# A hybrid attention/SSD trunk on one core: three projection units at the start instead of two, and three value units placed between the convolved projection groups

## The chip, the cores and the metric

One core of one Trainium2 chip runs the whole kernel. The metric is device time in microseconds (us) of one execution, the median of several runs. The engines are named as in the profile: PE is TensorE (PEld its weight loads), DVE is VectorE, ACT is ScalarE, POOL is GpSimd, SP issues the DMAs.

## What is computed

One layer of a streaming encoder for two groups of tokens that share the weights: 512 prompt tokens and 32 sample tokens, 544 in all, model width 1024. In float32:

```
h = rmsnorm(x)
[q, k, v | z, xBC, dt | gate_a, gate_b] = h @ w_in
ya = QK-normed chunk-band attention(q, k, v)
xBC = silu(causal depthwise conv of width 4 over xBC);  dt = softplus(dt + dt_bias)
yb = rmsnorm( SSD scan(xBC, dt) * silu(z) )
x += (sigmoid(gate_a) * (ya @ w_proj_a) + sigmoid(gate_b) * (yb @ w_proj_b)) @ w_out
x += ConvFFN(rmsnorm(x));   x += sigmoid(rmsnorm(x) @ w_ple_gate) * (p @ w_ple)
```

The outputs are y, the new keys and values, the SSD states and the convolution contexts of both groups.

## The kernel before, in words

Activations lie feature-major: a tile has 128 features on the partitions and 544 tokens along the free dimension. The dense work is cut into **units**: one unit makes 128 output features from 1024 input features and reads one weight tile of 128x1024 (all weights are packed on the host in the order in which the units use them, two units to a 1 MB DMA, `load`, tile `wr`). A unit has 8 **chunks**, one for each 128 input features. To keep float32 accuracy from the fast matmul form, a weight is split into `wh` (rounded) and `wl` (the rest), an activation into `hi` and `lo`, and a chunk (`mm3`) is 6 matmuls of 128x128 by 128x272: wh by hi, wh by lo and wl by hi, each for two halves of the tokens. `prep` makes `wh` on ACT (a copy that rounds) and `wl` on DVE, or for odd units below 40 on POOL; `wh` and `wl` have two buffers each.

`dense_steps` is the list of units, 192 in all: B, C and four x units of each of four groups ("xbc", with a convolution behind them), z, then q, k and v of eight head pairs, the gates, the output projections, the FFN and the last projection. `Dense.chunk` runs the next chunk and, after a unit's eighth, its epilogue; `dense.run(n)` runs n chunks, and the small matmuls of the SSD scan and of attention are put between chunks by hand (`ssd_a`, `ssd_b`, `att_a`, `att_b`, `att_c`). `dense.defer(n, fn)` runs fn n chunks later. PE's order is pinned to the order in which the program is written (`Ordered._pin`); the order of the other engines is set by a scheduler, which is bound by true dependencies and by the few `add_manual_dep` calls. On the chip each engine works through its own list in that order.

The PSUM banks: `dps` (two banks, two buffers) takes a dense unit, `sps` (one bank, four buffers) everything else. So a unit can't start before the unit two ahead of it has been read out by its epilogue.

**The start.** x comes in as eight tiles (`load_x`, tile `xin`), with the weights of units 0 and 1 in pieces between them. `split_g` makes hi on ACT and lo on DVE (L374, L375), `prep_part` the pieces of wh and wl (L259, L260). The sum of squares for the first rmsnorm is made apart from that: tiles 0 to 3 are squared and added on POOL (L443, L445), tiles 4 to 7 are squared on ACT and added on DVE. `Dense.start` runs units 0 and 1 together, chunk by chunk as the x tiles come; then `rstd_of` sums over the partitions with a matmul by ones (tile `rps`) and makes 1/rms on ACT (Ln, then Exp). The norm is not applied to h but to each unit's result: `evac_ext` multiplies it out of PSUM by `rstd`. Then `dt_product` (32 small matmuls, tile `dtp`), and 8 chunks later `dt_softplus`, 32 chunks after that `dt_sums`, whose result goes to DRAM (`asc`) and comes back spread over the partitions (`ab`) for the SSD scan. `bias_vector` writes a vector of relative-position biases to DRAM (`evec`), and 16 DMAs `bsc` of 320 KB spread it for attention.

**Epilogues.** `ep_xbc`: three DVE reads of PSUM into `ext` (L571, L573, L574), a convolution of one ACT and three DVE operations (tile `cv`), a tanh on ACT (`th`) and two last DVE operations into `bc` or `xs`. `ep_v`: one DVE read of PSUM into `v`, a DMA of v to DRAM, and three chunks later (`v_transpose`) five PE transposes of v (tiles `vt`, `vs`) and their copies on ACT.

The functions that the change touches, and their callers:

Of the kernel before, what the change touches and what calls it, by code (L numbers as in the profile page):

```python
# [15 lines left out]
D = 1024  # L16
# [100 lines left out]
def trunk(ctx: ExitStack, tc: tile.TileContext, a):  # L117
# [109 lines left out]

    raws = {0: r0}
    ready = {}
    first_rstd = []  # L230
    used = set()
# [8 lines left out]
    def prep(u):  # L240
        if u >= len(order) or u in ready or u in used:
            return
        load(u // 2)
        r = raws[u // 2][:, u % 2, :]
        hi = wp.tile([128, 1024], F32R, tag="wh", name="wh", bufs=2)
        lo = wp.tile([128, 1024], F32R, tag="wl", name="wl", bufs=2)
        ready[u] = (hi, lo)
        if u < 2:
            return r
        cp = S.copy(hi, r)  # L250
        if u == 3:
            tc.add_manual_dep(cp.ins, first_rstd[0].ins.name, ORDER, reason="order")
        eng = G if u < 40 and u % 2 == 1 else V
        eng.tensor_tensor(lo, r, hi.bitcast(F32), op=SUB)  # L254
        load(u // 2 + 1)

    def prep_part(u, r, c0, c1):
        hi, lo = ready[u]
        S.copy(hi[:, c0:c1], r[:, c0:c1])  # L259
        V.tensor_tensor(lo[:, c0:c1], r[:, c0:c1], hi[:, c0:c1].bitcast(F32), op=SUB)  # L260

# [26 lines left out]
    class Dense:  # L288
# [47 lines left out]
        def start(self):  # L336
            sts = self.steps[:2]
            pss = [dps() for _ in sts]
            ws = [next_unit(*units_of(st)[0]) for st in sts]
            for n in range(KD):  # L340
                for st, ps, w in zip(sts, pss, ws):
                    o = 128 * n
                    mm3(ps, w[0][:, o : o + 128], w[1][:, o : o + 128], *acts_of[st[0]](st)[n], n == 0, n == KD - 1)
                    self.count += 1
            self.i = 2
            first_rstd.append(rstd_of(rstd, acc, 1.0 / D))
            for st, ps in zip(sts, pss):
                epilogue[st[0]](ps, *st[1:])
            dt_product()

# [15 lines left out]
    def split(x):  # L366
# [3 lines left out]
        return hi, lo  # L370

    def split_g(x, g):
        hi, lo = slot(F32R, "hi"), slot(F32R, "lo")
        S.activation(hi, x, AF.Copy, scale=g)  # L374
        V.scalar_tensor_tensor(lo, x, g, hi.bitcast(F32), op0=MUL, op1=SUB)  # L375
        return hi, lo
# [15 lines left out]
    def rstd_of(dst, acc, scale, after=None):  # L392
# [3 lines left out]
        for h in range(2):  # L396
# [8 lines left out]
            if pre is not None:  # L405
                tc.add_manual_dep(ln.ins, pre.ins.name, ORDER, reason="table")
        for h in range(2):
            sl = slice(h * HALF, (h + 1) * HALF)
            last = S.activation(dst[:, sl], dst[:, sl], AF.Exp, scale=-0.5)
        return last  # L410

# [4 lines left out]
    for k in range(KD):  # L416
        hx.append(split_g(xt[k], vec[:, V_GMIX + k : V_GMIX + k + 1]))
        if k in (0, 1, 3):
            for u in range(2):
                prep_part(u, rw[u], (0, 256, 0, 512)[k], (256, 512, 0, 1024)[k])  # L420
    load(1)
    nc.sync.dma_start(hb, a["hb"].unsqueeze(0).to_broadcast([128, 2, 32]))
# [27 lines left out]
    done(acc2)  # L450
    rstd = big("rstd")
# [21 lines left out]
    def dt_product():  # L473
# [8 lines left out]
        for h in range(2):  # L482
            sl = slice(h * HALF, (h + 1) * HALF)
            V.tensor_tensor(dtx[:, sl], ps[h][:, :HALF], rstd[:, sl], op=MUL)
        dense.defer(8, lambda: dt_softplus(dtx))

    def dt_softplus(dtx):
# [23 lines left out]
        dt = tm[:, 0]  # L511
        V.scalar_tensor_tensor(dt, p, 2.0, x, op0=MUL, op1=ADD)
# [6 lines left out]
    def dt_sums(dtx, ws, r, dt, agf):  # L519
        cp = sps("cum")  # L520
# [761 lines left out]
```

## Time and profile before

| | |
|---|---|
| median of 3 runs | 1355.56 us (1354.17 to 1358.21) |
| the profiled execution | 1355.77 us |
| its span, first to last instruction | 1354.1 us |
| PE busy | 1338.2 us (99% of the span) |
| DVE, ACT, POOL busy | 852.6, 634.4, 313.7 us |
| granted TensorE clock, mean | 0.999 |
| idle PE time by the waits' view | 11.1 us in ten groups of waits, 4.1 us of it for `lo` at the start |

A row of a timeline view gives the start (us), the duration (us; of the whole merged group), the engine, the line and the operation, and in brackets how long the engine was idle before it and who ended that. A busy PE is not PE at its peak: its rows overlap, and the pace is read from the distance of their starts. The other engines' rows overlap a little too (by about 0.1 us).

### The profile page before, as it was taken

How to read it: one execution, taken by the hardware profiler on the slowest of the kernel's cores; microseconds unless marked ns; L12 is line 12 of the kernel's file. 1: busy time of each engine (PE TensorE's matmuls, PEld its weight loads, DVE VectorE, ACT ScalarE, POOL GpSimd, SP SyncE). 2: the span in 40 equal slices, each digit the busy share in tenths (PEclk: the TensorE clock that was granted, in tenths of full speed). 3: DMA queues.
4: the chain of work that ended last, by engine and by line, in shares of the span. 5: the costliest groups of instructions: out<-in, count | busy, mean ns of one | idle time of the engine just before them, and what ended most of it. 6: DMA issues, size and time to landing. Idle time of an engine off the chain costs nothing.

```text
span 1354.1 us, 26563 instructions
## 1 busy us (share of the span) xinstructions
PE 1338.2 (99%) x11045; PEld 1307.2 (97%) x11045; DVE 852.6 (63%) x1474; ACT 634.4 (47%) x1104; POOL 313.7 (23%) x442
## 2 busy tenths in 40 slices
PE   8999999999999999999999999999999999999998
PEld 7999998999999999999999999999999999999998
DVE  7999889755775656643554335677676356753545
ACT  5465555656676667542442223534444124432342
POOL 5456365544321211100000000133332013310000
PEclk9999999999999999999999999999999999999999
DMA  5733243332533332222223422222222232222231
GB/s 182 252 100 130 83 128 121 119 132 100 177 94 114 115 111 90 67 81 94 69 89 110 143 94 73 85 94 94 94 72 85 94 111 94 76 85 94 94 107 53
DMA packets 41896, 142.15 MB, mean 105 GB/s; under 512 B 9216, under 2 KB 13232, under 8 KB 29488
## 3 DMA queue, kind: packets, MB, share of 16 engines
q1 hardware_dynamic: 41776, 140.45, 31.4%
q8 instruction: 87, 1.43, 0.4%
q14 instruction: 33, 0.27, 0.1%
HBM read 129.27 MB, written 14.31 MB: 106 GB/s over the span
## 4 chain that ended last, share of the span: by engine, by line
PE 89%; DVE 6%; ACT 2%; DMA 1%; issue 1%; SPq 0%; POOL 0%; ACTq 0%; DVEq 0%; POOLq 0%
PE dps L130 80%; PE O L130 2%; PE yps L130 2%; PE L L130 1%; PE st L130 1%; DVE cv L599 1%; DVE qs L834 1%; PE Tp L133 1%; DVE wl L254 1%; PE xst L133 0%; PE gps L130 0%; DMA wr<-in_w 0%; DVE xs L603 0%; DMA ab<-asc 0%; PE qn L130 0%
## 5 line engine op out<-in xcount | busy, mean ns | idle before, releaser
L130 PE MATMUL dps<-hi,wh 128*128 128x272 f32 x2960 | 627.0, 293 | 0.6 <-DVE ext L574 0.4
L130 PE MATMUL dps<-lo,wh 128*128 128x272 f32 x2960 | 613.1, 288 | 4.1 <-DVE lo L375 4.1
L130 PE MATMUL dps<-hi,wl 128*128 128x272 f32 x2960 | 612.1, 288 | 0.0
L130 PEld LDWEIGHTS dps<-hi,wh 128*128 128x128 f32 x2960 | 466.0, 189 | 10.5 <-issue 7.8
L130 PEld LDWEIGHTS dps<-lo,wh 128*128 128x128 f32 x2960 | 465.9, 189 | 5.0 <-DVE lo L375 5.0
L130 PEld LDWEIGHTS dps<-hi,wl 128*128 128x128 f32 x2960 | 464.9, 188 | 0.0
L250 ACT CAST wh<-wr 128x1024 fp32r<-128x1024 f32 x192 | 201.2, 1048 | 386.0 <-PE dps L130 346.6
L254 DVE TENSOR_TENSOR wl<-wr,wh 128x1024 fp32r<-128x1024 f32 x173 | 213.6, 1235 | 47.6 <-ACT wh L250 42.3
L1033 DVE SCALAR_TENSOR_TENSOR ucv<-uext,vec,ucv 128x546 f32<-128x546 f32 x96 | 75.3, 784 | 4.4 <-ACT ucv L1030 2.7
L599 DVE SCALAR_TENSOR_TENSOR cv<-ext,hv,cv 128x547 f32<-128x547 f32 x72 | 71.0, 986 | 2.1 <-ACT cv L596 1.0
L1026 POOL COPY cfo<-uext 128x2 f32<-128x2 f32 x48 | 10.4, 217 | 261.7 <-DVE uext L573 261.7
L1023 POOL MEMSET uext<- 128x2 f32 x48 | 4.5, 95 | 278.7 <-issue 278.7
L1065 DVE TENSOR_TENSOR x<-x,dps 128x544 f32<-128x544 f32 x24 | 17.3, 721 | 78.0 <-PE dps L130 78.0
L571 DVE TENSOR_TENSOR uext<-dps,rstd 128x272 f32<-128x272 f32 x48 | 21.3, 443 | 63.0 <-PE dps L130 58.3
L785 DVE CUSTOM_DVE_ANT_0 P<-L,bias 128x128 f32<-128x128 f32 (+3 forms) x64 | 30.8, 481 | 46.1 <-PE L L130 41.6
L254 POOL TENSOR_TENSOR wl<-wr,wh 128x1024 fp32r<-128x1024 f32 x19 | 48.4, 2549 | 43.9 <-ACT wh L250 42.4
L1027 POOL COPY cfo<-uext 128x2 f32<-128x2 f32 x48 | 55.5, 1157 | 0.0
L787 ACT ACTIVATE P<-P,sm 128x128 f32<-128x128 f32 (+3 forms) x64 | 36.0, 562 | 26.8 <-DVE sm L785 26.4
L660 POOL TENSOR_TENSOR ab<-ab,bc 128x512 f32<-128x512 f32 (+1 forms) x28 | 37.0, 1325 | 40.7 <-ACT ab L659 40.7
L368 ACT CAST hi<-me 128x544 fp32r<-128x544 f32 x24 | 15.5, 647 | 61.9 <-DVE me L1051 61.9
L1030 ACT ACTIVATE ucv<-uext,vec 128x546 f32<-128x546 f32 x48 | 40.7, 847 | 7.2 <-DVE uext L574 2.6
L650 ACT ACTIVATE m<-ab,tm 128x128 f32<-128x128 f32 x128 | 40.8, 389 | 6.3 <-DMA ab<-asc 6.2
(243 smaller groups left out, 1548.9 us busy)
## 6 DMA issues: line engine op xcount, KB each, us to landing
wr<-in_w SPq DMA_DIRECT2D x96, 1024.0 KB, 4.9
ab<-asc SPq DMA_DIRECT2D x32, 256.0 KB, 5.1
bsc<-evec SPq DMA_DIRECT2D x16, 320.0 KB, 8.0
bias<-bsc SPq DMA_DIRECT2D x16, 256.0 KB, 3.2
xin<-in_xT SPq DMA_DIRECT2D x8, 272.0 KB, 5.7
out_o_v<-v SPq DMA_DIRECT2D x8, 272.0 KB, 3.2
out_o_k<-qk SPq DMA_DIRECT2D x8, 272.0 KB, 2.9
x<-in_xT SPq DMA_DIRECT2D x8, 272.0 KB, 4.4
```

The costliest lines, as they stand in the source:

```text
L130: return self._pin(nc.tensor.matmul(*args, **kw))
L250: cp = S.copy(hi, r)
L254: eng.tensor_tensor(lo, r, hi.bitcast(F32), op=SUB)
L571: V.tensor_tensor(ext[:, n : n + HALF], ps[:, 0, :HALF], rstd[:, 0:HALF], op=MUL)
L599: V.scalar_tensor_tensor(y[:, :n], ext[:, j : j + n], hv[:, 24 * j + ti : 24 * j + ti + 1], y[:, :n], op0=MUL, op1=ADD)
L650: S.activation(m[:, i], ab[:Q, i], AF.Relu, scale=-1.0, bias=tm[:Q, 1, c, hd : hd + 1])
L660: G.tensor_tensor(ab, ab, cc[:, tk].unsqueeze(1).to_broadcast([128, H, Q]), op=MUL)
L785: V.tensor_tensor_reduce(out=P, in0=L, in1=B, scale=1.0, scalar=3e38, op0=ADD, op1=MIN, accum_out=nm[:n])
L787: S.activation(P, P, AF.Exp, scale=-1.0, bias=nm[:n], accum_out=sm[:n])
L1027: G.tensor_copy(cfo[:, i, 2:4], ext[:, UW - 2 : UW])
L1030: S.activation(y[:, :n], ext[:, 0:n], AF.Identity, scale=vec[:, V_FW + i : V_FW + i + 1], bias=vec[:, V_FB + i : V_FB + i + 1])
L1033: V.scalar_tensor_tensor(y[:, :n], ext[:, j : j + n], vec[:, V_FW + 48 * j + i : V_FW + 48 * j + i + 1], y[:, :n], op0=MUL, op1=ADD)
```

## The change

- **Third unit at the start.** `Dense.start` takes three units. Units 0 and 1 run chunk by chunk as before; all 8 chunks of unit 2 follow. Unit 2's weights come with the second weight DMA (`r1`), now issued right behind the x tiles; its wh and wl have tiles of their own (`prep_third`), its sums two `sps` banks (`dpa`, `dpb`). The matmul `rps` of the norm stands behind the sixth chunk of unit 2.
- **Sum of squares.** All eight squares are on ACT and all sums on DVE, none on POOL; tile 0 is squared early, tiles 1 to 7 are ordered behind the split of unit 2's weights. That split is ordered behind the last x split.
- **Epilogues of units 0 to 2**: all three are read out of PSUM first, and then convolved.
- **Later work.** `dt_product` goes four chunks behind the start (it followed at once), `dt_softplus` 6 chunks after it (8), `dt_sums` 26 after that (32); the first operation of `bias_vector` is ordered behind the last one of `dt_softplus`. `wl` of unit 3 is made on DVE, not on POOL.
- **Order of units.** The value units of head pairs 0 and 1 are units 6 and 7, ahead of the second xbc group, that of pair 2 is unit 14, between the second and the third; z(0) comes behind the fourth xbc group. The counts at which the SSD scan and attention are put between the chunks stay.

The core of the diff:

```diff
@@ dense_steps
     def qkv(m):
-        return [("qk", m, 0), ("qk", m, 1), ("v", m)]
+        return [("qk", m, 0), ("qk", m, 1)] + [("v", m)] * (m >= 3)
...
-    p += proj(1) + proj(2) + z(0) + proj(3) + z(1)
+    p += v(0, 1) + proj(1) + v(2) + proj(2) + proj(3) + z(0) + z(1)
@@ loads
     for k in range(5, KD):
         load_x(k)
+    r1 = wp.tile([128, 2, 1024], F32, tag="wr", name="wr", bufs=2)
+    nc.sync.dma_start(r1, a["w"][1])
     nc.sync.dma_start(vec[:, V_BG:V_N], a["vec"][:, V_BG:V_N])
@@ prep
-        eng = G if u < 40 and u % 2 == 1 else V
+        eng = G if 3 < u < 40 and u % 2 == 1 else V
...
+    def prep_third():
+        third.extend(slot(F32R, n) for n in ("wh", "wh", "wl", "wl"))
+        ready[2] = Joined(*third[:2]), Joined(*third[2:])
+        return [prep_part(2, r1[:, 0, :], c, c + 512) for c in (0, 512)][-1]
@@ Dense.start
+            sts = self.steps[:3]
+            pss = [dps() for _ in range(2)]
...
+            pss.append(Banks(sps("dpa"), sps("dpb")))
...
+            seq = [(n, i) for n in range(KD) for i in range(2)] + [(n, 2) for n in range(KD)]
+            for j, (n, i) in enumerate(seq):
...
+                self.count += 1
+                if j == 21:
+                    rstd_of(rstd, acc, 1.0 / D)
+            done(*third)
+            self.i = 3
+            for f in [xbc_evac(ps, *st[1:]) for st, ps in zip(sts, pss)]:
+                f()
+            self.defer(4, dt_product)
@@ the sum of squares
+        if k == 0:
+            sq0 = S.activation(acc, xt[0], AF.Square)
+            tc.add_manual_dep(sq0.ins, part[0].ins.name, ORDER, reason="order")
+    last_w = prep_third()
+    tc.add_manual_dep(last_w[0].ins, last[0].ins.name, ORDER, reason="order")
...
-    acc2 = slot(name="acc2")
-    for k in range(KD):
-        if k < 4:
-            q = acc2 if k == 0 else eslot("sq")[:, :T]
-            G.tensor_tensor(q, xt[k], xt[k], op=MUL)
-            if k > 0:
-                G.tensor_tensor(acc2, acc2, q, op=ADD)
...
+    for k in range(1, KD):
+        q = eslot("sq")[:, :T]
+        sq = S.activation(q, xt[k], AF.Square)
+        add = V.tensor_tensor(acc, acc, q, op=ADD)
+        tc.add_manual_dep(sq.ins, last_w[0].ins.name, ORDER, reason="order")
+        tc.add_manual_dep(add.ins, last_w[1].ins.name, ORDER, reason="order")
@@ dt_product, dt_softplus, bias_vector
-        dense.defer(8, lambda: dt_softplus(dtx))
+        dense.defer(6, lambda: dt_softplus(dtx))
...
-        dense.defer(32, lambda: dt_sums(dtx, ws, r, dt, agf))
+        dense.defer(26, lambda: dt_sums(dtx, ws, r, dt, agf, last_dt))
...
+        neg = V.tensor_scalar(er[0:16, 0:257], er[0:16, 0:257], -1.0, None, op0=MUL)
+        tc.add_manual_dep(neg.ins, last_dt.ins.name, ORDER, reason="order")
```

`xbc_evac` is the first half of the old `ep_xbc` (up to the reads of PSUM), and returns the second (`xbc_conv`).

How the order of the engines changes, at the three places that the prediction speaks of. Line numbers of the changed program are some 2 to 37 higher than those of the program before.

DVE at the start, before: `lo` of an x tile, `wl` of units 0 and 1 and then of unit 2, the sums `acc`, up to the first read of a unit out of PSUM (`ext`).

```order
L375 SCALAR_TENSOR_TENSOR lo<-xin,vec,hi 128x544 x3
L384 TENSOR_TENSOR acc<-acc,sq 128x544
L459 TENSOR_SCALAR hv<-vec 128x120
L460 TENSOR_SCALAR hv<-vec 128x16
L461 TENSOR_SCALAR hv<-vec 128x1
L375 SCALAR_TENSOR_TENSOR lo<-xin,vec,hi 128x544
L448 TENSOR_TENSOR acc<-acc,acc_200 128x544
L375 SCALAR_TENSOR_TENSOR lo<-xin,vec,hi 128x544
L384 TENSOR_TENSOR acc<-acc,sq 128x544 x2
L254 TENSOR_TENSOR wl<-wr,wh 128x1024
L571 TENSOR_TENSOR ext<-dps,rstd 128x272
```

DVE at the start, now:

```order
L409 SCALAR_TENSOR_TENSOR lo<-xin,vec,hi 128x544 x5
L490 TENSOR_SCALAR hv<-vec 128x16
L491 TENSOR_SCALAR hv<-vec 128x1
L262 TENSOR_TENSOR wl<-wr,wh 128x512 x2
L477 TENSOR_TENSOR acc<-acc,sq 128x544 x5
L256 TENSOR_TENSOR wl<-wr,wh 128x1024
L477 TENSOR_TENSOR acc<-acc,sq 128x544
L256 TENSOR_TENSOR wl<-wr,wh 128x1024
L477 TENSOR_TENSOR acc<-acc,sq 128x544
L488 TENSOR_SCALAR hv<-vec 128x120
L602 TENSOR_TENSOR ext<-dps,rstd 128x272 x2
```

The five last `lo` stand together, `wl` of units 2 (two halves) and 3 and 4 (128x1024) stand between them and the last sums, and `ext` comes behind all of these.

PE at the third chunk behind unit 6, the first value unit, now (dps rows are dense matmuls, three rows to a chunk; `vt` and `vs` are the transposes of v, `cum` begins `dt_sums`):

```order
L133 MATMUL dps<-hi,wh 128x272 x2
L133 MATMUL dps<-lo,wh 128x272 x2
L133 MATMUL dps<-hi,wl 128x272 x2
L136 MATMUL vt<-ident,v 128x128 x4
L136 MATMUL vs<-ident,v 32x128
L133 MATMUL dps<-hi,wh 128x272 x2
L133 MATMUL dps<-lo,wh 128x272 x2
L133 MATMUL dps<-hi,wl 128x272 x2
L133 MATMUL cum<-dtt,tri 128x128
```

The transposes of v stood some 220 chunks later before; they now stand three chunks behind unit 6, one chunk ahead of `dt_sums`.

DVE ahead of the read of unit 6 (`v<-dps`), now (`dtt` and `tm` are the softplus, `er` and `e` the bias vector):

```order
L538 SCALAR_TENSOR_TENSOR dtt<-dtt 128x160
L636 SCALAR_TENSOR_TENSOR cv<-ext,hv,cv 128x547
L539 SCALAR_TENSOR_TENSOR dtt<-dtt 128x160
L636 SCALAR_TENSOR_TENSOR cv<-ext,hv,cv 128x547
L542 SCALAR_TENSOR_TENSOR tm<-dtt 128x160
L584 TENSOR_SCALAR er<-er 16x257
L256 TENSOR_TENSOR wl<-wr,wh 128x1024
L636 SCALAR_TENSOR_TENSOR cv<-ext,hv,cv 128x547
L545 SCALAR_TENSOR_TENSOR dtt<-tm,ea 128x160
L586 COPY e_899<-er 16x383
L800 TENSOR_TENSOR v<-dps,rstd 128x544
```

Behind the epilogues of units 0 to 5 and the whole softplus stands the read of v; before, the seventh read of a unit out of PSUM stood at this place, and no PE instruction but the second unit after it waited for that.

## Rows read from the trace of the kernel before

**Rows 1.** Who waited for whom on PE: total us, times, longest.

```profile
PE dps L130 <- DVE lo L375: 4.1, 3, 3.3
PE st L130 <- DVE xs L690: 1.8, 2, 1.2
```

**Rows 2.** Timeline of PE at the start.

```profile
16.15 0.55 PE L130 MATMUL dps<-lo,wh 128*128 128x272 f32 x2 [3.27 <-DVE lo L375]
...
20.05 0.41 PE L130 MATMUL dps<-lo,wh 128*128 128x272 f32 x2
...
25.07 1.08 PE L130 MATMUL rps<-acc,ones 128*128 128x272 f32 x4
26.08 2.04 PE L130 MATMUL dtp<-xin,dtw 128*32 128x272 f32 x32
...
34.67 1.15 PE L130 MATMUL tps<-sel,dtx 128*128 128x32 f32 x10
```

**Rows 3.** Stretches of 5 us: busy us (instructions) of each engine, PEclk, DMA share, GB/s.

```profile
15.00:20.00 5.00, 3.85 (x18) 3.85 (x19) 5.00 (x8) 2.11 (x5) 3.94 (x5) 0.66 0.99 383
```

**Rows 4.** Timeline of DVE at the start.

```profile
14.24 4.70 DVE L375 SCALAR_TENSOR_TENSOR lo<-xin,vec,hi 128x544 fp32r<-128x544 f32 x3
...
19.77 0.77 DVE L375 SCALAR_TENSOR_TENSOR lo<-xin,vec,hi 128x544 fp32r<-128x544 f32 x1
20.46 0.71 DVE L448 TENSOR_TENSOR acc<-acc,acc 128x544 f32<-128x544 f32 x1
...
25.35 1.23 DVE L254 TENSOR_TENSOR wl<-wr,wh 128x1024 fp32r<-128x1024 f32 x1 [2.01 <-ACT wh L250]
27.02 0.44 DVE L571 TENSOR_TENSOR ext<-dps,rstd 128x272 f32<-128x272 f32 x1 [0.45 <-ACT rstd L409]
```

**Rows 5.** Timeline of POOL at the start.

```profile
13.73 1.78 POOL L445 TENSOR_TENSOR acc<-acc,sq 128x544 f32<-128x544 f32 x1
```

**Rows 6.** Timeline of ACT at the start.

```profile
11.32 1.47 ACT L374 ACTIVATE hi<-xin,vec 128x544 fp32r<-128x544 f32 x2
...
13.87 0.64 ACT L383 ACTIVATE sq<-xin 128x544 f32<-128x544 f32 x1
...
24.27 1.05 ACT L250 CAST wh<-wr 128x1024 fp32r<-128x1024 f32 x1 [6.13 <-PE dps L130]
```

**Rows 7.** DMA issues of 11.3 to 11.6 us: operation, count, KB, us to landing.

```profile
wr<-in_w SPq DMA_DIRECT2D x1, 1024.0 KB, 6.4
```

**Rows 8.** Timeline of DVE from 28 to 59 us.

```profile
28.34 2.58 DVE L555 COPY e<-er 16x383 f32<-16x383 f32 x1
...
31.20 2.41 DVE L599 SCALAR_TENSOR_TENSOR cv<-ext,hv,cv 128x547 f32<-128x547 f32 x3
...
34.34 0.69 DVE L603 SCALAR_TENSOR_TENSOR bc<-th,cv 128x512 f32<-128x512 f32 x1
...
45.26 1.76 DVE L508 SCALAR_TENSOR_TENSOR dtt<-dtt 128x160 f32<-128x160 f32 x1
...
55.76 2.92 DVE L599 SCALAR_TENSOR_TENSOR cv<-ext,hv,cv 128x547 f32<-128x547 f32 x1
58.60 0.31 DVE L515 SCALAR_TENSOR_TENSOR dtt<-tm,ea 128x160 f32<-128x160 f32 x1
58.84 0.43 DVE L571 TENSOR_TENSOR ext<-dps,rstd 128x272 f32<-128x272 f32 x1
```

**Rows 9.** Timeline of POOL: a weight subtraction, the second of three before 58 us.

```profile
42.96 3.88 POOL L254 TENSOR_TENSOR wl<-wr,wh 128x1024 fp32r<-128x1024 f32 x1 [2.53 <-ACT wh L250]
```

**Rows 10.** Timeline of PE: `dt_sums` begins behind unit 6; an SSD wait.

```profile
59.96 0.56 PE L130 MATMUL cum<-dtt,tri 128*128 128x128 f32 x4
...
232.68 1.10 PE L130 MATMUL st<-wj,bt 128*128 128x512 f32 x2 [1.16 <-DVE xs L690]
```

**Rows 11.** Instructions on tile v, 28 to 345 us: ns min/median/max, first and last start.

```profile
L763 DVE TENSOR_TENSOR v<-dps,rstd x3: 723/724/725, 286.3 to 338.3; 128x544 f32<-128x544 f32 x3
```

**Rows 12.** Timeline of SP: the DMAs of the bias rows.

```profile
34.38 14.32 SPq L563 DMA_DIRECT2D bsc<-evec  x14
```

More of the change, by code (lines that the diff above doesn't have):

```diff
@@ L45, in qkv, with v @@
     def qkv(m):
-        return [("qk", m, 0), ("qk", m, 1), ("v", m)]
+        return [("qk", m, 0), ("qk", m, 1)] + [("v", m)] * (m >= 3)
+    def v(*ms):
+        return [("v", m) for m in ms]
     p = proj(0)
-    p += proj(1) + proj(2) + z(0) + proj(3) + z(1)
+    p += v(0, 1) + proj(1) + v(2) + proj(2) + proj(3) + z(0) + z(1)
     for m in range(NPAIR):
@@ L225, in trunk @@
     done(wz_t)
-    raws = {0: r0}
+    raws = {0: r0, 1: r1}
     ready = {}
-    first_rstd = []
     used = set()
@@ L249, in prep @@
             return r
-        cp = S.copy(hi, r)
-        if u == 3:
-            tc.add_manual_dep(cp.ins, first_rstd[0].ins.name, ORDER, reason="order")
-        eng = G if u < 40 and u % 2 == 1 else V
+        S.copy(hi, r)
+        eng = G if 3 < u < 40 and u % 2 == 1 else V
         eng.tensor_tensor(lo, r, hi.bitcast(F32), op=SUB)
@@ L258, in prep_part, with __init__, __getitem__ @@
         hi, lo = ready[u]
-        S.copy(hi[:, c0:c1], r[:, c0:c1])
-        V.tensor_tensor(lo[:, c0:c1], r[:, c0:c1], hi[:, c0:c1].bitcast(F32), op=SUB)
+        return (S.copy(hi[:, c0:c1], r[:, c0:c1]),
+                V.tensor_tensor(lo[:, c0:c1], r[:, c0:c1], hi[:, c0:c1].bitcast(F32), op=SUB))
+    class Joined:
+        def __init__(self, *t):
+            self.t = t
+        def __getitem__(self, k):
+            c0, c1 = k[1].start, k[1].stop
+            return self.t[c0 // 512][k[0], c0 % 512 : c0 % 512 + c1 - c0]
+    class Banks:
+        def __init__(self, *t):
+            self.t = t
+        def __getitem__(self, k):
+            return self.t[k[1]][k[0], k[2]]
+    third = []
+    def prep_third():
+        third.extend(slot(F32R, n) for n in ("wh", "wh", "wl", "wl"))
+        ready[2] = Joined(*third[:2]), Joined(*third[2:])
+        return [prep_part(2, r1[:, 0, :], c, c + 512) for c in (0, 512)][-1]
     pos = [0]
@@ L336, in start @@
         def start(self):
[L337 to L349, printed above, removed]
+            sts = self.steps[:3]
+            pss = [dps() for _ in range(2)]
+            ws = [next_unit(*units_of(st)[0]) for st in sts[:2]]
+            pss.append(Banks(sps("dpa"), sps("dpb")))
+            pos[0] += 1
+            used.add(2)
+            ws.append(ready.pop(2))
+            seq = [(n, i) for n in range(KD) for i in range(2)] + [(n, 2) for n in range(KD)]
+            for j, (n, i) in enumerate(seq):
+                w = ws[i]
+                o = 128 * n
+                mm3(pss[i], w[0][:, o : o + 128], w[1][:, o : o + 128], *acts_of[sts[i][0]](sts[i])[n], n == 0,
+                    n == KD - 1)
+                self.count += 1
[6 more added lines that the diff above has]
+            self.defer(4, dt_product)
         def run(self, n):
@@ L370, in split @@
         return hi, lo
+    last = []
     def split_g(x, g):
         hi, lo = slot(F32R, "hi"), slot(F32R, "lo")
-        S.activation(hi, x, AF.Copy, scale=g)
-        V.scalar_tensor_tensor(lo, x, g, hi.bitcast(F32), op0=MUL, op1=SUB)
+        last[:] = (S.activation(hi, x, AF.Copy, scale=g),
+                   V.scalar_tensor_tensor(lo, x, g, hi.bitcast(F32), op0=MUL, op1=SUB))
         return hi, lo
@@ L406, in rstd_of @@
                 tc.add_manual_dep(ln.ins, pre.ins.name, ORDER, reason="table")
[L407 to L410, printed above, removed]
+            S.activation(dst[:, sl], dst[:, sl], AF.Exp, scale=-0.5)
     hx = []
@@ L419, in trunk @@
             for u in range(2):
-                prep_part(u, rw[u], (0, 256, 0, 512)[k], (256, 512, 0, 1024)[k])
-    load(1)
+                part = prep_part(u, rw[u], (0, 256, 0, 512)[k], (256, 512, 0, 1024)[k])
+        if k == 0:
[3 more added lines that the diff above has]
+    tc.add_manual_dep(last_w[0].ins, last[0].ins.name, ORDER, reason="order")
     nc.sync.dma_start(hb, a["hb"].unsqueeze(0).to_broadcast([128, 2, 32]))
@@ L458, in trunk @@
     hv = const.tile([128, 138], F32, name="hv")
-    V.tensor_scalar(hv[:, 0:120], vec[:, V_CW : V_CW + 120], 0.5, None, op0=MUL)
+    hv0 = V.tensor_scalar(hv[:, 0:120], vec[:, V_CW : V_CW + 120], 0.5, None, op0=MUL)
+    tc.add_manual_dep(hv0.ins, add.ins.name, ORDER, reason="order")
     V.tensor_scalar(hv[:, 120:136], vec[:, V_BG : V_BG + 16], 0.5, None, op0=MUL)
@@ L511, in dt_softplus @@
         dt = tm[:, 0]
-        V.scalar_tensor_tensor(dt, p, 2.0, x, op0=MUL, op1=ADD)
+        last_dt = V.scalar_tensor_tensor(dt, p, 2.0, x, op0=MUL, op1=ADD)
         ea = const.tile([128, 32], F32, name="ea")
@@ L516, in dt_softplus, with dt_sums @@
         agf = ag.rearrange("p c h -> p (c h)")
-        dense.defer(32, lambda: dt_sums(dtx, ws, r, dt, agf))
-    def dt_sums(dtx, ws, r, dt, agf):
+        dense.defer(26, lambda: dt_sums(dtx, ws, r, dt, agf, last_dt))
+    def dt_sums(dtx, ws, r, dt, agf, last_dt):
         cp = sps("cum")
@@ L548, in dt_sums, with bias_vector @@
         done(dtx, *ws)
-        dense.defer(4, bias_vector)
-    def bias_vector():
+        dense.defer(4, lambda: bias_vector(last_dt))
+    def bias_vector(last_dt):
         er, e0 = slot(name="er"), slot(name="e0")
         nc.sync.dma_start(er[0:16, 0:257], a["rb"])
-        V.tensor_scalar(er[0:16, 0:257], er[0:16, 0:257], -1.0, None, op0=MUL)
+        neg = V.tensor_scalar(er[0:16, 0:257], er[0:16, 0:257], -1.0, None, op0=MUL)
+        tc.add_manual_dep(neg.ins, last_dt.ins.name, ORDER, reason="order")
         V.tensor_copy(e0[0:16, 0:383], er[0:16, 0:1].to_broadcast([16, 383]))
@@ L580, in ep_xbc, with xbc_evac @@
     def ep_xbc(ps, kind, i):
+        xbc_evac(ps, kind, i)()
+    def xbc_evac(ps, kind, i):
         if kind == "x":
@@ L593, in ep_xbc, with xbc_conv @@
         G.tensor_copy(cso[:, ti, 3:6], ext[:, XW - 3 : XW])
+        return lambda: xbc_conv(ext, ti, dst)
+    def xbc_conv(ext, ti, dst):
         n = XW - 3
```

5 lines of the change are left out of this document (removed).

## The prediction

> **What bounds the kernel now.** PE is busy for 99% of the span (the page's first section), so a change can only give back, or add, idle PE time, or time at a low clock. The first view to read is therefore who waited for whom on PE: the largest entry is 4.1 us for `lo` at the start, the next 1.8 us for `xs` of the SSD scan [rows 1]. The timeline of PE shows the first in place: one wait of 3.27 us ahead of 16.15 us [rows 2]. Behind it the nine pairs of matmuls from 16.15 to 20.05 take 3.9 us, where the twenty pairs from 20.05 to 25.07 take 0.251 us each: 3.9 less 9 x 0.251 is 1.6 us lost, and the granted clock is 0.66 in that stretch [rows 3], half the full 2.4 GHz (1.2 GHz) for most of it.
>
> Why `lo` was late is read from DVE: three `lo` took 4.70 us, while a later one took 0.77 [rows 4]. In those 4.70 us POOL was adding squares [rows 5]; the 0.77 us one ran with POOL idle. I take POOL as the cause. Last comes the stretch behind the start: DVE works there almost without a gap up to its read of unit 5 at 58.84 [rows 8], whereas PE is by then nearly through unit 6 (`dt_sums` begins at 59.96 [rows 10]). PE had ended unit 5 at about 53.8 (34.67 [rows 2] for unit 2, 1.1 for `tps`, three units of 24 pairs, 6.02 each), so DVE reads it 5 us late. That costs nothing before, since only the second unit after it needs the bank, 6 us on; the change puts an instruction on PE that needs it sooner.
>
> **The start: a gain of 3.3 us.** No squares remain on POOL, so `lo` takes 0.77 us [rows 4] and each x tile is split as it lands. The last late one is tile 3: its `hi` starts at 11.32 as before, takes 0.75 (half of the pair in [rows 6]), its `lo` is there at 12.9. From there PE has 29 pairs of units 0 and 1 left, 7.3 us at 0.251; with 0.1 for the first one, they end at 20.3, not at 25.07. I assume that the clock stays full, since the waits left are under 0.6 us.
>
> Unit 2 gives the cover for the norm: six chunks, 4.5 us, up to 24.8, where `rps` stands. The sums aren't ready then. The second weight DMA was issued at 11.31 and landed at 17.7 [rows 7]; it is now ahead of three small loads (337 KB, 0.9 us at the 383 GB/s of this stretch [rows 3]), so 16.8. The squares stand behind the rounding of unit 2's weights: 1.15 us (two halves of a 1.05 us copy [rows 6]), then six squares at 0.55 apart (0.64 each, less 0.1 overlap), then unit 3's rounding 1.0: 22.5. On DVE, by the order shown, `wl` of unit 3 (1.2 [rows 4]), a sum (0.65), `wl` of unit 4 (1.15) and the last sum (0.7) follow: 26.1. PE waits 1.3 us there. From `rps` to the first read of a unit took 27.02 less 25.07, 1.95 us; so DVE begins to read at 28.1, and the four operations that free unit 0's banks (0.44 [rows 4] and less each) end at 29.3. PE has finished unit 2 at 28.7 and waits 0.6. So units 0 to 2 and `rps` are done and unit 3 starts at 29.3; with the 2.04 us of `dtp`, still to come, 31.4. Before, the same work was done at 34.67 [rows 2]. The bounds: 4.7 if the 1.3 us wait goes (the weights land earlier), 1.7 if the clock falls as before (1.6 us).
>
> **The value unit 0: a loss of 4.3 us.** Unit 6 is now a value unit, and three chunks behind it stand the transposes of v. PE gets there at 29.3 + 2.04 + 1.1 (`tps` [rows 2]) + 4 units of 6.02 + 2.26 (9 pairs) = 58.8. DVE must by then have read v. I take DVE's time from the stretch before: from its first read to that of unit 5 it took 58.84 - 27.02 = 31.8 us [rows 4, 8]. By the order shown it now does the same between the first read and that of v, and one more unit's epilogue: 0.8 for the reads, 2.3 for three `cv` (2.41 with overlap) and 0.7 for `bc` or `xs` [rows 8], 3.8 in all. It is held by two weight subtractions of POOL, not three (unit 3's went to DVE, ahead of this stretch). What one costs is seen in three rows: a copy that took 2.58 where its neighbours take 0.3, an operation of 1.76 among ones of 0.3, a `cv` of 2.92 for 0.78 [rows 8], each while POOL subtracted [rows 9]; 2.3, 1.4 and 2.1, so 1.9 on average. The first two tanhs have nothing to cover them now, 0.7 more. 28.1 + 31.8 + 3.8 - 1.9 + 0.7 = 62.5, and with v's own 0.72 [rows 11] 63.2. Before that, the read of unit 5 comes 0.3 after PE wants its bank for unit 7. So PE arrives at 59.1, waits 4.0 for v, and 0.3 is lost ahead of it. The second value unit is free of this: DVE catches up in the 4 us. The third has a pair of SSD steps' matmuls between it and its transposes, and lighter work on DVE ahead.
>
> The trace gives the block of 1.4 to 2.3 us whichever engine came first. The Trainium skill (SBUF — State Buffer, Who interferes with whom) says that a DVE instruction with two SBUF inputs and a POOL instruction that reads SBUF exclude each other, and that the one that starts first holds the ports for the whole instruction. The POOL row of 3.88 us, longer than the others, agrees with blocks in both directions. By that rule a POOL subtraction that loses costs DVE nothing, and the wait for v would be near zero: that is the rival of DVE in time, below.
>
> **The clock behind that wait: a loss of 0.8 us.** The 3.27 us wait was followed by 1.6 us lost to the low clock; the wait of 1.16 [rows 10] by none. 4.0 is nearer to the first, but 30 us of dense work lie ahead of it here and not there, so I take half, and keep 0 and 1.6.
>
> **The SSD waits: a gain of 1.3 us.** Both waits for `xs`, 0.66 and 1.16 us [rows 1, 10], come while DVE is behind. Two value units in place of xbc units take 2 x 3.4 us of epilogue off DVE ahead of the first, so that one should go; the second comes after as many xbc units as before, so I count half of it. Bounds: 0 and 1.8.
>
> **Free edits.** The bank pair `dpa`, `dpb` and the joined weight tiles add no instruction on PE. `wl` of unit 3 on DVE is in the chain above. The bias vector moves off the start, where DVE had room, to just ahead of v's read; it was inside the 31.8 us already. Its 16 DMAs come some 30 us later, beside the SSD's first loads (a rival below). The later q and k units have 25 chunks or more before attention reads them.
>
> **The sum.** -3.3 + 4.3 + 0.8 - 1.3 = +0.5 us on the profiled execution of 1355.77, whose span is 1354.1; it lies 0.2 above the median of the runs. So 1356.1: no change that a measurement of this kernel can tell, which is about 0.3% (4.1 us, 1351.5 to 1359.6).
>
> **The rivals.** *DVE in time for v.* If DVE wins the ports, or the scheduler's order leaves less ahead of v's read than I count, the wait of 4.0 and its clock term go: -3.3 + 0.3 - 1.3 = -4.3, 1351.3. For it: without the POOL blocks DVE would be done at 59.4, 0.3 after PE. Against: all three subtractions in that stretch did hold DVE. Chance 0.25, half of it beyond the 0.3%.
>
> *The SSD loads behind the bias rows* (slower). SP issues eight `bsc` DMAs ahead of `asc`, eight more, two stores of v and a weight load ahead of the first `ab`. Fourteen of them took 14.32 us [rows 12]. They now begin 1.5 us behind the bias vector, at about 64; 16 at 1.02 and 4 us for the rest put `ab` at 85. Its first DVE reader stands behind the read of unit 9, at about 85 too. What waits behind that is the read of unit 10, which PE wants for unit 12 at about 97, and some 6 us of DVE work lie between. So PE is held from an `ab` at 91 on, that is from 1.4 us for each `bsc`; at 1.7 us it costs 4.2 us: 1360.3. Chance 0.10.
>
> *The start doesn't gain*: the weights of unit 2 land later than 16.8, and each microsecond moves `rps` and everything behind it by one. At 20 the 3.3 us are gone: 1359.4. Against it: PE has 4.5 us of unit 2 to run only if they have landed by 20, and the DMAs are fed in order. Chance 0.07.
>
> **How the numbers follow.** My forecast, 0.58, has bounds of its own from -2.5 (a small wait for v, no clock loss) to +3.5 (full clock loss, no SSD relief): 1353 to 1359. To hold 8 in 10 the range takes in most of the first rival: 1350.8 to 1359.3. Faster by over 0.3%: half of 0.25 and 0.05 from the tails, 0.17. Slower: most of the slower rival, and 0.01 of the third, 0.08. Within: 0.75.
>
> **What would show it.** In the profile after: `lo` at about 0.77 us each, units 0 and 1 done near 20.3; a PE wait of about 1.3 us ahead of `rps` and 0.6 ahead of unit 3; a wait of about 4 us on PE ahead of `vt` near 59 us, released by the DVE read of v, perhaps with a low clock behind it; the SSD wait near 100 us gone. Wrong if the transposes of v start without a wait (then faster), if `lo` stays long without POOL, or if ACT and DVE stand waiting for `ab` near 85 us.

## The result: 1.1% slower, and the profile after

The changed kernel takes 1370.25 us (median of 4 runs, 1369.29 to 1373.02), the kernel before 1355.96 beside it: ratio 1.0106, 95% interval 1.0089 to 1.0123. That is 14.3 us slower, and 11 us above the predicted range. The profiled execution took 1369.29 us. From the page of the changed kernel, its first section:

```profile
span 1367.6 us, 26568 instructions
...
PE 1342.5 (98%) x11045; PEld 1309.7 (96%) x11045; DVE 845.3 (62%) x1479; ACT 641.1 (47%) x1111; POOL 304.2 (22%) x434
```

The span grew by 13.5 us. PE's busy time grew by 4.3 us (1338.2 before) with the same number of matmuls; I put that down to the clock, whose granted mean fell from 0.999 to 0.994. The other 9.2 us are idle PE time. The chief waits of PE, in the form of [rows 1] (us in total, times, the longest):

```profile
PE st L133 <- DVE xs L727: 7.1, 2, 4.7
PE vt L136 <- DVE v L800: 3.6, 1, 3.6
PE rps L133 <- DVE acc L477: 1.6, 1, 1.6
PE Ts L136 <- DVE Ps L826: 1.4, 1, 1.4
PE dps L133 <- DVE ext L605: 1.4, 2, 0.7
```

The 4.1 us for `lo` are gone and `xs` of the SSD scan has taken their place, with 7.1 us. Where these waits stand, in the timeline of PE after, beside [rows 2, 10]:

```profile
26.69 1.16 PE L133 MATMUL rps<-acc,ones 128*128 128x272 f32 x4 [1.64 <-DVE acc L477]
...
30.07 0.49 PE L133 MATMUL dps<-hi,wh 128*128 128x272 f32 x2 [0.72 <-DVE ext L605]
...
33.24 2.04 PE L133 MATMUL dtp<-xin,dtw 128*32 128x272 f32 x32
...
58.39 0.49 PE L133 MATMUL dps<-hi,wh 128*128 128x272 f32 x2 [0.63 <-DVE ext L605]
...
64.50 1.12 PE L136 MATMUL vt<-ident,v 128*128 128x128 f32 x4 [3.61 <-DVE v L800]
...
102.83 1.12 PE L133 MATMUL st<-wj,bt 32*128 32x512 f32 x2
108.67 2.05 PE L133 MATMUL st<-wj,bt 128*128 128x512 f32 x2 [4.72 <-DVE xs L727]
...
117.34 0.38 PE L133 MATMUL cbt<-bc 128*128 128x128 f32 x2
...
245.22 1.87 PE L133 MATMUL st<-wj,bt 128*128 128x512 f32 x2 [2.42 <-DVE xs L727]
```

The same three matmuls of the SSD scan, in the timeline of PE before:

```profile
97.89 1.12 PE L130 MATMUL st<-wj,bt 32*128 32x512 f32 x2
99.67 1.10 PE L130 MATMUL st<-wj,bt 128*128 128x512 f32 x2 [0.66 <-DVE xs L690]
...
106.63 0.38 PE L130 MATMUL cbt<-bc 128*128 128x128 f32 x2
```

Between the first and the last of these three the kernel before took 8.74 us, the changed one 14.51 (117.34 less 102.83): 5.8 us are lost here alone. Its wait of 4.72 replaces one of 0.66, 4.1 of the 5.8; the rest is low clock, which the windows show (columns: window and its length, then busy time and count of PE, PEld, DVE, ACT and POOL, the granted clock, the DMA share, GB/s):

```profile
0.00:20.00 20.00, 17.49 (x111) 16.43 (x112) 11.85 (x22) 13.60 (x23) 3.61 (x19) 1.00 0.86 301
60.00:80.00 20.00, 16.39 (x120) 15.16 (x119) 8.50 (x22) 4.86 (x13) 3.63 (x4) 0.91 0.72 225
100.00:120.00 20.00, 15.28 (x129) 13.09 (x128) 17.38 (x34) 9.72 (x20) 9.04 (x12) 0.83 0.28 93
240.00:250.00 10.00, 7.58 (x64) 5.53 (x61) 8.10 (x15) 5.97 (x14) 6.58 (x4) 0.83 0.34 119
```

Reading all such distances in the same way gives the account of the 13.5 us; in each row the low clock is what is left of the loss when the waits are taken off:

| place | us | from |
|---|---|---|
| start, up to `tps` | -2.4 | `tps` at 39.83 for 34.67 [rows 2], with ten chunks (7.53 us) more done |
| 57 to 70 us | +5.8 | waits of 0.63 and 3.61; 1.6 of low clock |
| SSD scan, 103 to 112 us | +5.8 | 4.72 for 0.66; 1.7 of low clock |
| SSD scan, 245 us | +2.9 | 2.42 for 1.16 [rows 10]; 1.6 of low clock |
| the rest | +1.4 | by difference; `Ts`, the first transposes of attention, waits 1.4 |

The wait at 108 us is followed back through DVE and SP. SP, its own queue of DMA issues:

```profile
65.38 5.06 SPq L594 DMA_DIRECT2D bsc<-evec  x8
...
72.54 2.01 SPq L594 DMA_DIRECT2D bsc<-evec  x3
...
77.03 2.18 SPq L594 DMA_DIRECT2D bsc<-evec  x3
79.31 0.53 SPq L241 DMA_DIRECT2D wr<-in_w  x1
79.89 1.48 SPq L594 DMA_DIRECT2D bsc<-evec  x2
81.41 5.35 SPq L682 DMA_DIRECT2D ab<-asc  x3
```

The sixteen `bsc` rows go out between 65.4 and 81.4, and the SSD loads `ab` stand behind them. The view of DMA issues from 60 to 100 us says what the DMAs moved in each microsecond (its row of GB/s) and how long each issue took to land (the last column, us):

```profile
GB/s 352 0 17 0 25 265 46 205 233 333 320 236 305 358 336 201 363 260 331 319 300 314 315 293 321 359 401 377 309 209 186 187 227 434 389 289 150 16 0 8
...
bsc<-evec SPq DMA_DIRECT2D x16, 320.0 KB, 6.6
...
ab<-asc SPq DMA_DIRECT2D x4, 256.0 KB, 7.9
...
ab<-asc SPq DMA_DIRECT2D x1, 128.0 KB, 10.6
```

DVE is at the first reader of `ab` at 88.1, and stands:

```profile
87.95 0.18 DVE L605 TENSOR_TENSOR ext<-dps,rstd 128x32 f32<-128x32 f32 x1
92.07 0.41 DVE L689 TENSOR_TENSOR m<-ab,tm 32x256 f32<-32x256 f32 x1 [3.94 <-DMA ab<-asc]
...
101.70 5.43 DVE L636 SCALAR_TENSOR_TENSOR cv<-ext,hv,cv 128x547 f32<-128x547 f32 x3
...
107.82 1.74 DVE L727 SCALAR_TENSOR_TENSOR xs<-xs,vec,yps 128x32 f32<-128x32 f32 x8
```

From there DVE is behind; one group of three `cv` takes 5.43 us (2.43 at 31.0 us) while POOL works almost without a pause from 101.6 to 106.6 us, and `xs`, for which PE waits, is made only at 107.82.

### The profile page after: what moved, and what is told of

It is laid out like the page before. It is cut to its first block, busy times and chain, and to the rows that moved or that the text cites. A ratio compares the mean times of both kernels' runs of the same rounds, so it can differ in the third digit from the quotient of the medians.

```text
span 1367.6 us, 26568 instructions
## 1 busy us (share of the span) xinstructions
PE 1342.5 (98%) x11045; PEld 1309.7 (96%) x11045; DVE 845.3 (62%) x1479; ACT 641.1 (47%) x1111; POOL 304.2 (22%) x434
## 4 chain that ended last, share of the span: by engine, by line
PE 86%; DVE 8%; DMA 3%; ACT 2%; issue 1%; SPq 1%; POOL 0%; ACTq 0%; DVEq 0%
PE dps L133 76%; DVE cv L636 2%; PE O L133 2%; PE yps L133 2%; PE st L133 1%; PE L L133 1%; DVE qs L871 1%; DMA ab<-asc 1%; PE Tp L136 1%; DVE wl L256 1%; DMA bsc<-evec 1%; DMA wr<-in_w 1%; SPq L594 1%; PE xst L136 0%; PE gps L133 0%
## 5 line engine op out<-in xcount | busy, mean ns | idle before, releaser
L256 POOL TENSOR_TENSOR wl<-wr,wh 128x1024 fp32r<-128x1024 f32 x18 | 44.5, 2473 | 34.0 <-ACT wh L254 32.8
```

## The experiments

Each is compared with the kernel before on the same chip; ratios carry their 95% interval. In what follows a kernel's waits are those of its own profiled execution.

**1. The transposes of v later.** The changed kernel, with

```diff
-        dense.defer(3, lambda: v_transpose(m, v))
+        dense.defer(10 if m < 3 else 3, lambda: v_transpose(m, v))
```

> The changed kernel, with the transposes of the first three value units 10 chunks behind the unit instead of 3. Theory: two stalls, one behind the other. The first (PE waits 3.6 us for v near 60 us, and runs at half clock behind it) goes; but the second is bound by DMAs, the spread sums ab, which land at 92 us however early PE comes, so PE now waits longer there: 1366 to 1370 us, and the wait of PE for xs near 105 us, 4.7 before, is over 6. Rival: the two are independent, and the gain of the first stays: 1364 to 1365.

1364.23 us, ratio 1.0046 (1.0029 to 1.0064). The number fell where the rival put it, but not for its reason: PE still stands 2.0 us at 61 us, now for `cum`, whose input on DVE is late too, so the wait for v alone was worth 1.6. The larger gain came from SP: with v's transposes moved, `asc` and the first `ab` are placed among the `bsc` rows instead of behind them, DVE's first read of `ab` stands at 85.99 (92.07) and waits 0.84 us (3.94), and the wait at 108 us is gone. The one near 237 us is still there, 2.3 us.

**2. The bias vector early.** The changed kernel, with

```diff
-        tc.add_manual_dep(neg.ins, last_dt.ins.name, ORDER, reason="order")
+        tc.add_manual_dep(neg.ins, hv0.ins.name, ORDER, reason="order")
```

> The changed kernel, with the bias vector ordered behind the start's sums as before, not behind the softplus; so the 16 bias DMAs go out near 30 us. Theory: they are what makes ab late; ab lands by 85 us, DVE has no wait for it, the PE wait for xs near 105 us falls from 4.7 to under 1 and its half clock goes: 1370.3 less 5.8, 1363 to 1365. Rival: DVE's load in the new order of units makes xs late: the wait stays at 4 us or more, 1369 to 1371.

1365.57 us, ratio 1.0057 (1.0039 to 1.0076), 0.6 above the theory's range. The `bsc` rows now go out from 29.7 us on, the small `ab` lands 5.5 us after its issue (10.6), and PE has no wait at 108 us:

```profile
ab<-asc SPq DMA_DIRECT2D x1, 128.0 KB, 5.5
```

So the bias rows were the cause of that wait. What was not expected is that the low clock behind the wait for v grew: the 65 to 70 us window is at a granted clock of 0.50 (0.71 in the changed kernel).

**3. Both.**

> Both edits: transposes of the value units 10 chunks late, bias vector early. Theory: both stalls go and nothing takes their place; what stays is the start's gain of 2.4 us, the longer wait near 245 us with its clock (2.9) and 1.2 in attention: 1356 to 1359. Rival: DVE's load is the cause and shows up elsewhere: 1363 or more.

1365.97 us, ratio 1.0065 (1.0047 to 1.0083). The theory failed: two of the places were gone and most of the loss was still there. The number is where the rival put it; experiments 7 to 9 show another cause than DVE's load. PE's timeline shows where, a wait of 2.42 us that has become one of 4.63:

```profile
241.56 2.05 PE L133 MATMUL st<-wj,bt 128*128 128x512 f32 x2 [4.63 <-DVE xs L727]
```

**4. The order of units alone**, in the kernel before:

```diff
-        return [("qk", m, 0), ("qk", m, 1), ("v", m)]
+        return [("qk", m, 0), ("qk", m, 1)] + [("v", m)] * (m >= 3)
...
-    p += proj(1) + proj(2) + z(0) + proj(3) + z(1)
+    p += v(0, 1) + proj(1) + v(2) + proj(2) + proj(3) + z(0) + z(1)
```

> The kernel before, with the new order of units alone (start, sums of squares and bias vector as before). Theory: the wait for v comes with the order (DVE reads units 4 to 5 us late there, the transposes want v after 2.3): 3 to 4 us and 1.6 of clock near 60 us; no wait over 1.5 us near 100 us, since the bias DMAs are early; 2.9 near 235: 1362 to 1366. Rival: the order alone is harmless and the stalls come from the start: 1354 to 1358.

1362.82 us, ratio 1.0038 (1.0024 to 1.0052). The number is in the theory's range, but not for its first reason: the transposes of the first value unit wait 0.34 us here, since PE is later at that point (those of the third, near 128 us, 0.68). The wait for v needed the new start. But 2.2 us of wait for `xs` near 237 us and 1.3 for `Ts` near 360 are there without the new start or the late bias vector. These two belong to the order of units. They are not the whole loss: of the ten executions the one at a mean granted clock of 1.000 took 1358.58 us, the five at 0.995 or 0.996 took 1362.7 to 1364.0, so low clock has a part in it, and where that was lost the one kept trace (0.998) doesn't show.

**5, 6. The start without the new order**, with the bias vector late as in the change, and early:

```diff
-        return [("qk", m, 0), ("qk", m, 1)] + [("v", m)] * (m >= 3)
+        return [("qk", m, 0), ("qk", m, 1), ("v", m)]
...
-    p += v(0, 1) + proj(1) + v(2) + proj(2) + proj(3) + z(0) + z(1)
+    p += proj(1) + proj(2) + z(0) + proj(3) + z(1)
```

> The changed start, sums of squares, epilogues and late bias vector with the old order of units (z(0) and the value units where they were). Theory (the losses belong to the unit order, each at its own place: the wait for v, the store of the convolution contexts ahead of the SSD loads near 230 us, the attention start): only the start's gain and the late bias rows are left; the rows are put partly behind the first SSD load here, so 1353 to 1357, with the waits at 230 and 360 us as before. Rival (the bias rows hold the SSD loads whatever the unit order): a PE wait of 3 us or more for xs near 100 us and 1358 to 1362.

> As the run with the start alone, and the bias vector is made early again (ordered behind the last sum of squares and its first scaling, not behind softplus). Theory: nothing but the start's gain of 2.4 to 3.3 us is left: 1353.0 to 1355.0, faster than before by 0.1 to 0.3%. Rival (the start leaves DVE behind by what PE gains, and the gain is given back at the SSD waits for xs): 1356 to 1358, with waits for xs that are longer than before by about 2 us.

1362.26 us, ratio 1.0044 (1.0029 to 1.0059), and 1358.71, ratio 1.0012 (1.0002 to 1.0021). Both theories missed: the new start by itself is no gain. The waits near 237 and 360 us are back to what they were before, as the theory had it, but the rival is right that the start is given back, and wrong about where. The timeline of PE in the run with the early bias vector:

```profile
58.36 0.49 PE L133 MATMUL dps<-hi,wh 128*128 128x272 f32 x2 [0.63 <-DVE ext L605]
...
63.38 0.66 PE L133 MATMUL cum<-dtt,tri 128*128 128x128 f32 x4 [1.77 <-DVE dtt L545]
```

The windows behind that wait (columns as above):

```profile
60.00:65.00 5.00, 3.23 (x21) 2.63 (x20) 4.81 (x12) 1.57 (x3) 0.84 (x2) 0.89 0.15 62
65.00:70.00 5.00, 5.00 (x23) 4.27 (x23) 3.65 (x9) 1.34 (x6) 1.76 (x3) 0.50 0.06 14
```

PE waits 0.63 us for a read of `ext` and 1.77 for the last product of softplus, then runs the next five microseconds at half clock (0.50). DVE explains it: its first read of a unit stands at 28.69 us, where it stood at 27.02 before [rows 4], and from there to 63 us it hardly pauses. PE came 2.4 us earlier, DVE 1.7 us later. With the late bias vector the profiled execution shows the same waits (its span is 0.3 us longer), while its median is 3.6 us higher; the wait for `xs` near 103 us, where the rival of the first run put 3 us or more, is 0.95 and 0.77. What the late vector costs in the median isn't seen in the trace, which is that of the fastest of six executions, with a granted clock of 0.997; the two slowest, 1364.4 and 1365.9 us, have 0.994. So a part of it is low clock at a place that wasn't recorded, and the cause stays open.

**7. z(0) back**, in the kernel of experiment 3:

```diff
-    p += v(0, 1) + proj(1) + v(2) + proj(2) + proj(3) + z(0) + z(1)
+    p += v(0, 1) + proj(1) + v(2) + proj(2) + z(0) + proj(3) + z(1)
```

> The run with both edits (value transposes 10 chunks late, bias vector early), and z(0) back between the third and the fourth xbc group. Theory (what is left of the loss comes from the last xbc unit being one unit earlier against the SSD steps, so that SP stops at the store of the convolution contexts ahead of the next two SSD loads, PE wait 4.6 us plus low clock near 240 us): with the last xbc unit later that wait falls to 1.2 us or less, and the time to 1359 to 1363. Rival (DVE is simply fuller between 150 and 240 us with two value units gone from there): the wait stays over 2 us somewhere in that stretch, 1364 to 1367.

**8. The store of the convolution contexts later**, in the kernel of experiment 1 (`hp_out` collects the state stores):

```diff
-        nc.sync.dma_start(a["o_cs"], cso)
+        cs_out = nc.sync.dma_start(a["o_cs"], cso)
+        tc.add_manual_dep(cs_out.ins, hp_out[-1].ins.name, ORDER, reason="order")
```

> The run with the value transposes 10 chunks late, and one edit more: the store of the convolution contexts is ordered behind the last state store on SP. Theory (that store holds SP for 4.8 us and ACT then waits 4.6 us for the SSD load): ACT's wait for that load goes, the PE wait of 2.3 us near 237 us falls to under 1.2 and its low clock (1.7 us) with it: 1361 to 1363. Rival (DVE is the bound there, 92 to 95% busy between 150 and 230 us): the wait stays at 2 us or more, 1363.5 to 1365.

1361.29 us, ratio 1.0034 (1.0023 to 1.0044), and 1360.95, ratio 1.0032 (1.0018 to 1.0047): both theories held (the second number is 0.05 under its range), and the two edits, which have nothing else in common, take away the same wait. SP's DMA issues in experiment 1:

```profile
221.75 0.34 SPq L747 DMA_DIRECT2D out_o_hp<-h  x1
227.01 0.34 SPq L959 DMA_DIRECT2D out_o_cs<-cso  x1
227.44 0.86 SPq L682 DMA_DIRECT2D ab<-asc  x2
```

The same place of SP in experiment 8:

```profile
221.14 0.34 SPq L748 DMA_DIRECT2D out_o_hp<-h  x1
221.57 0.87 SPq L683 DMA_DIRECT2D ab<-asc  x2
```

In experiment 1 the store `out_o_cs` stands ahead of two `ab`, and waits 4.8 us for POOL's last copy into `cso`; ACT then stands for `ab`:

```profile
230.74 1.28 ACT L687 ACTIVATE m<-ab,tm 128x128 f32<-128x128 f32 x4 [4.59 <-DMA ab<-asc]
```

In experiment 8 the loads go out at 221.57, ACT reads them at 225.44 without a wait, and PE's wait of 2.3 us is no longer there. In the kernel before, the two loads went out at 220.25 and the store at 231.99. The new order ends the convolved units one unit earlier, and that puts the store ahead of the loads.

**9. All three edits in the changed kernel** (transposes late, bias vector early, contexts late), its unit order kept:

> The changed kernel, its unit order kept, with three edits: value transposes 10 chunks late, bias vector early, convolution contexts stored behind the last state. Theory (each of the three was one place of loss, the one at 240 us being the store ahead of the SSD loads): the 4.6 us wait for xs near 240 us that the first two edits left falls to under 1.2, 1359 to 1361.5; left over are the wait for cum near 61 us and the one for Ps near 360 us. Rival (DVE too full between 150 and 240 us): a wait of 3 us or more stays there, 1364 to 1367.

1360.24 us, ratio 1.0027 (1.0013 to 1.0040), as the theory had it: 10 us of the 14.3 were these three couplings. Left over are 1.8 us for `cum` and 1.5 for `Ts`.

**10. The value unit of pair 2 back** behind its q and k, in the kernel of experiment 9 (`m >= 2` for `m >= 3`, and no `v(2)`):

> The three edits, and the value unit of head pair 2 back behind its q and k. Theory (without that unit the norm of the last k falls between the tanhs of z, ACT loads its tables twice more, 1.28 us each, and the first softmax is late for PE): five table loads between 250 and 520 us become three, the PE wait for Ps of 1.7 to 2.1 us near 360 us goes, 1.5 to 3 us less than with the three edits alone. Rival (the table loads are hidden, the softmax is late because attention starts on more units of q and k): the wait stays over 1 us and the time within 1 us of the three edits alone.

ACT from 250 to 520 us in experiment 9 has five table loads, as in the changed kernel (three in the kernel before), three of them in some eight microseconds:

```profile
289.26 1.28 ACT L767 ACT_TABLE_LOAD   x1
...
348.96 1.28 ACT L757 ACT_TABLE_LOAD   x1
...
353.69 1.28 ACT L790 ACT_TABLE_LOAD   x1
...
355.87 1.28 ACT L825 ACT_TABLE_LOAD   x1
...
379.02 1.28 ACT L767 ACT_TABLE_LOAD   x1
```

In experiment 10 three are left, and the wait for `Ts` is gone, so the mechanism is the one named: without v(2) as a spacer the norm of the last k (logarithm) falls behind the first tanh of z, and ACT changes tables twice more. The Trainium skill (ScalarE: Activation LUTs, Table sets: the hidden batching unit) advises to group calls by table set; the trace agrees that each change costs a load, but at 1.28 us, where the page has about 2.7. The size fell short: 1359.03 us, ratio 1.0022 (1.0011 to 1.0033), 1.2 us less and not 1.5 to 3, and since the intervals of experiments 9 and 10 overlap, the wait's going is shown, but no gain of time. Its profiled execution has a new wait of 0.9 us for `xs` at 299 us, with low clock behind it (0.63 from 300 to 305 us).

**11, 12. `dt_sums` four chunks later**, in the kernel of experiment 6 and in that of experiment 10:

```diff
-        dense.defer(26, lambda: dt_sums(dtx, ws, r, dt, agf, last_dt))
+        dense.defer(30, lambda: dt_sums(dtx, ws, r, dt, agf, last_dt))
```

> The new start with the old unit order and the early bias vector, and dt_sums 30 chunks after dt_softplus instead of 26. Theory (the start's 2.4 us are given back at about 61 us, where PE stands 1.8 us at the matmul cum for the last product of softplus on DVE, with up to 3.4 us of low clock behind it; DVE itself is only late for that one matmul): the wait for cum goes and the low clock with it, 0.6 us for one read of ext stays: 1354.0 to 1356.0, 1.8 to 5 us under the run without this edit. Rival (DVE is the bound from 29 to 63 us, and whatever PE puts first there waits for it): the 1.8 us turn up at the next bank that DVE has to read, 1357.5 to 1359.5.

> All the edits of this study at once: value transposes late, bias vector early, convolution contexts late, value unit 2 behind its q and k, and dt_sums 30 chunks after dt_softplus. Theory (the losses are separate places): what is left is the start's gain less 0.6 us, so 1354 to 1356.5, not slower than the kernel before. Rival (DVE is the bound between 29 and 63 us): as with the edits without dt_sums, 1357 to 1360.

1353.09 us, ratio 0.9976 (0.9967 to 0.9985), and 1353.80, ratio 0.9983 (0.9973 to 0.9993). Both are faster than the kernel before, and by a little more than the theories gave (0.9 and 0.2 us under their ranges); without this one number the ratios were 1.0012 and 1.0022. The wait for `cum` is gone and nothing near it has taken its place, as PE's timeline of experiment 11 shows:

```profile
58.10 0.49 PE L133 MATMUL dps<-hi,wh 128*128 128x272 f32 x2 [0.57 <-DVE ext L605]
...
64.21 0.56 PE L133 MATMUL cum<-dtt,tri 128*128 128x128 f32 x4
```

Its windows, beside those of experiment 6:

```profile
60.00:65.00 5.00, 5.00 (x41) 4.83 (x40) 4.71 (x12) 1.72 (x3) 0.91 (x2) 1.00 0.11 46
65.00:70.00 5.00, 5.00 (x41) 4.60 (x40) 4.96 (x9) 2.23 (x5) 4.14 (x4) 1.00 0.25 42
```

So DVE was late for that one matmul, not the bound of the stretch; its backlog shows only in the 0.57 us for `ext`. The version of experiment 11 (new start, old order, bias vector early, `dt_sums` later) beats both kernels. Experiment 12, which has the new places of z(0) and of the first two value units, is no faster: nothing here shows a gain from the new order of units.

## Why the prediction was wrong, point by point

**The start: right, sized at -3.3, measured -2.4.** With no squares on POOL five `lo` in a row took 3.62 us, where three had taken 4.70 [rows 4]; PE's waits for them fell to 0.9 us in all, units 0 and 1 ended at 20.4 (20.3 predicted), the clock stayed at 1.00. PE waited 1.64 ahead of `rps` (1.3) and 0.72 ahead of unit 3 (0.6); `rps` came at 26.7 instead of 26.1, and that is most of the 0.9. The gain is there up to `tps`; experiments 5 and 6 show that it was given back at 61 us, which the prediction did not have.

**The value unit: right in place and wait, 4.3 and 0.8 predicted, 5.8 measured.** PE waited 0.63 for `ext` (0.3), 3.61 for v (4.0), and lost 1.6 to the clock, the upper bound. DVE read v at 63.74 where I had 62.5. Two POOL subtractions stretched a `cv` each to 2.63 and 2.93 us, as assumed. What I did not see is that the same stretch makes `cum` late: without v ahead of it, PE waits 1.8 to 2.0 us there (experiments 1, 6, 9). So the value unit itself adds some 1.6 us of wait; the rest is DVE's being late for whatever wants it at that point, and experiments 5 and 6 have it without any value unit. The rival *DVE in time for v* did not occur.

**The SSD waits: the step that failed.** I took 1.3 us off, because two value units relieve DVE. They do: from 60 to 80 us DVE is busy for 8.5 us of the 20, before for 19.35:

```profile
60.00:80.00 20.00, 20.00 (x161) 19.20 (x160) 19.35 (x40) 9.70 (x18) 7.38 (x16) 1.00 0.41 134
```

But DVE's work there was not the limit, the load was, and instead of a gain the first of the two waits cost 5.8 us with the clock. I had the cause among the rivals, *the SSD loads behind the bias rows*, with 0.10 and up to 4.2 us, and the sign that I had named for it came: DVE stands for `ab` from 88.1 to 92.07. The step that made it look unlikely is the arrival of `ab` at 85: I counted SP's issues (16 at 1.02 us, about what they took, and 4 us for the rest), and nothing for the bytes that are still on their way. The first `ab` went out at 81.4, sooner than I reckoned, but landed 10.6 us later. An estimate from the row of GB/s in the view of DMA issues: of the 7.0 MB issued from 61 us on, 4.6 had moved by 81.4, so 2.4 MB of bias rows and weights stood ahead of it, 7 us at the 293 to 401 GB/s that followed. DVE read it at 92.07, past the 91 from which I had said that it counts. The path was wrong there too: by the rival's rule that is 1.1 us, at the bank for unit 12; the wait came later, at `xs`, with the stretched `cv` group in between. That its price was near the rival's 4.2 is luck.

**What no step had.** "The counts at which the SSD scan and attention are put between the chunks stay" was taken as costing nothing. It means that every unit stands elsewhere against them: the store of the contexts came ahead of two SSD loads (2.9 us at 245, experiments 3, 7, 8), and the norm of a k came between tanhs (a wait of 1.4 us near 370, experiments 4, 10). I had checked the later q and k units only for being ready in time. The order of SP and of ACT on either side of these places would have shown both.

The sum by the same steps with their measured sizes: -2.4 + 5.8 + 5.8 + 2.9 + 1.4 = 13.5, where the 1.4 is the remainder of the account; that it equals the wait for `Ts` was not tested apart.

## What to carry to other kernels

When units move against work that stays at fixed counts, walk the in-order queues (SP's DMA issues, ACT's table sets) at every place that stays, not only where the moved unit lands; a store that waits for its data stops every load behind it. For a load behind bulk transfers, reckon with the bytes ahead of it, not with the issues. And a gain at the start is kept only if the slower engine's due dates move with it: here one deferral count decided between 1.0012 and 0.9976.

## What was not expected of the hardware

The low clock behind a wait was not fixed by its length. The wait for `cum` near 61 us was 1.8 to 2.0 us in eight profiled executions; the window from 65 to 70 us behind it has a granted clock of 0.50 in three of them (experiments 3, 5, 6), 0.67 in one (experiment 1), and 1.00 in four (experiments 7 to 10). At 0.50, which is 1.2 GHz, a stretch of five microseconds does half its work, so the same wait costs 2 us or 5. The times of all executions say the same: of the twelve of experiment 6 the two at a mean granted clock of 1.000 took 1354.5 and 1356.4 us, the six at 0.997 took 1359.0 to 1360.3. So a median of such a kernel depends on how many of its executions lost the clock, and the 1.0012 of experiment 6 holds both kinds. In experiment 11, where the wait is gone, the clock of these windows is 1.00, and no execution is under 0.998. What decides between these was not tried.
